# Five plain pairs instead of seven, one product packed into three PSUM banks, D folded into C and 7, and eight adds on GpSimd

## The chip, the cores and the metric

The kernel runs on one core of a Trainium2 chip. The metric is the time of one execution on the device in microseconds, lower is better. The span in a profile goes from the first to the last instruction of one profiled execution; the execution's own time is a little longer.

The engines are called as in the profile: PE (TensorE, matrix products, with PEld for its weight loads), DVE (VectorE), ACT (ScalarE), POOL (GpSimd) and SP (SyncE, which here only issues transfers). Every engine works through its own instructions in their order and waits on semaphores for the others.

## The reference

```python
def setup_inputs():
    batch, m, k, n = 16, 512, 1024, 768
    return {
        "input": np.random.randn(batch, m, k).astype(np.float32),
        "grad_output": np.random.randn(batch, m, n).astype(np.float32),
    }

def reference(input, grad_output):
    grad_weight = np.einsum('bmk,bmn->kn', input, grad_output)
    return grad_weight.astype(np.float32)
```

Both inputs are seen as matrices X of 8192 x 1024 and G of 8192 x 768, and the result is X transposed times G, 1024 x 768, in float32.

## The kernel before

**Tiles.** The 8192 rows are cut into 64 slabs of 128 rows, and two slabs make a pair, so there are 32 pairs (`u`, 0 to 31). The result is cut into four quadrants of 512 x 384: A (upper left), B (upper right), C (lower left), D (lower right). Each quadrant has four blocks of 128 x 384 (`q`, 0 to 3), so A2 is the third block of A. One product is a matmul of a 128x128 weight tile and a 128x384 moving tile in bf16, which adds into a PSUM bank.

**Two kinds of pairs** (`LOADS`, line 12). A plain pair `s` needs for each slab the four quadrants' four blocks, so 32 products in all. A pair `P` treats its two slabs and the two halves of X's and G's columns as 2 x 2 block matrices and multiplies them by Winograd's form of Strassen's scheme, with seven products instead of eight, so 28 products of the same size. These seven are named 1, 5, 6, 7, A, B and C; their results go to sums of their own (`macc` for 1, 5, 6, 7), and A, B and C share the sum with the plain pairs. D gets products from plain pairs alone. The scheme needs sums of operands: six DVE instructions a pair in bf16, three for X (`sum_x`, lines 183 to 187, tokens x0, x1, x2) and three for G (`sum_g`, lines 193 to 197, tokens g0, g1, g2). Before, pairs 0 to 5 and pair 31 are plain and 25 are `P`.

**Loads.** POOL issues nearly all loads before everything else, in the order of the pairs: G's tile (line 152), then X's (line 153), cast from float32 to bf16 on the way. Fourteen pairs fit at once. The first slabs come as float32 through SP and ACT and are rounded by DVE and ACT (line 201), so that PE can start early. Ahead of that a few warm-up matmuls (line 135) run on constants.

**Blocks and banks.** PSUM has eight banks, and a block in work holds one. There are 32 sums of 128 x 384, so blocks are carried in and out. `multiply` (line 277) runs some products of a block; `close` (line 297) takes a bank's sum to SBUF, by an ACT copy (token c, line 327), or by DVE (token v: a copy at line 329, or an add onto the sum so far at line 331); `fill` (line 265) has ACT copy a sum back into a bank (token f, line 274), after which products add onto it. The four blocks of A stay in banks 7, 4, 1 and 3 until near the end; the rest rotates over banks 0, 2, 5 and 6.

**The end.** The quadrants are put together from the products when a block is closed for the last time (lines 304 to 312): 6 takes 1, 7 takes 6, A takes 1, C takes 7; 5 is closed by two subtractions (lines 307 and 309), and B and D take what these leave. A finished quadrant block of 192 KB is stored by SP (line 320); the very last block, B3, lies in two banks, 256 and 128 columns, and its second part is stored through ACT's queue.

**What sets the order.** `PLAN` (line 17) is a list of tokens, computed ahead of time and written out. The loop at line 336 goes through it, and each engine gets its instructions in the order of the tokens. `C2@0.1` is one product of C2, opened in bank 0; `A1.3` three more of A1; `fC1@3` fills C1 into bank 3; `cB1` and `vB1` close B1; `x0.6` is the first X sum of pair 6; `r0` to `r4` are roundings. The token's place among the others is no clock: only the order on each engine and the semaphores count.

Of the kernel before, what the change touches and what calls it, by code (L numbers as in the profile page):

```python
# [11 lines left out]
LOADS = "ssssssPPPPPPPPPPPPPPPPPPPPPPPPPs"  # L12

PLAN = (
    "A0@7.1 A3@3.1 A1@4.1 C3@5.1 C2@0.1 C1@2.1 r0 cC3 C0@6.1 vC2 A2@1.1 cC1 D0@5.1 vC0 B0@0.1 cD0 D1@2.1 "
    "r1 r3 B3@6.1 r2 D3@5.2 vB0 r4 A1.1 A2.1 cD1 vB3 A3.1 B1@0.2 cD3 B2@2.2 vB1 D2@6.2 cB2 C0@5.1 C1@0.1 "
    "vD2 A0.1 fD0@2 A2.1 vC0 A3.1 fD1@6 A1.1 D0.2 vC1 C2@5.2 cD0 D1.2 vC2 C3@0.2 cD1 B0@2.2 vC3 B3@5.3 "
    "fB1@6 vB0 A0.2 fB2@0 vB3 B1.2 fC0@2 B2.2 cB1 C1@5.2 vB2 C0.2 fD2@6 A3.1 vC1 D3@0.2 cC0 D2.2 fC2@5 "
    "vD3 C3@2.1 A1.1 cD2 A2.1 vC3 C2.1 B0@0.1 D1@6.1 vC2 D0@2.1 vB0 fD2@5 A3.2 vD1 A1.2 fB0@0 D2.2 vD0 "
    "B1@6.2 cD2 B0.2 vB1 B2@2.2 cB0 B3@5.2 vB2 C0@6.2 fC1@0 A2.2 vB3 fC2@2 C1.2 vC0 C3@5.2 cC1 C2.2 vC3 "
    "fD0@6 A0.2 D1@0.4 vC2 D3@5.4 vD1 D0.4 vD3 C3@2.2 vD0 B3@5.2 C0@0.2 vC3 fC1@6 A3.2 vB3 fB2@2 A0.2 vC0 "
    "C1.2 fD2@5 B2.2 cC1 D2.2 vB2 C2@0.2 cD2 B0@6.2 vC2 fB1@2 A1.4 vB0 fC1@0 B1.4 C2@5.2 cB1 D2@6.2 vC2 "  # L30
    "C1.2 fD0@2 A2.4 vD2 fD3@5 vC1 fC3@6 D0.2 D3.2 vD0 C3.2 cD3 C0@0.2 vC3 B2@2.4 vC0 fB3@6 B0@5.4 vB2 "
    "fD1@0 B3.4 fC0@2 vB0 A3.1 g0.6 fB1@5 A3.3 vB3 A0.2 g1.6 A0.2 fC1@6 D1.1 g2.6 D1.3 A2.2 vD1 A1.3 x0.6 "
    "fC2@0 C0.3 C1.1 x1.6 C1.2 cC0 C2.1 x2.6 C2.2 cC1 C3@2.1 g0.7 C3.2 cC2 B1.3 fD0@6 vC3 D2@0.2 g1.7 cB1 "
    "D0.2 vD2 fD3@2 A2.1 A3.1 A0.1 g2.7 cD0 10@5.1 D3.2 c10 x0.7 11@0.2 cD3 12@6.2 v11 13@5.2 c12 50@2.1 "
    "x1.7 50.1 c13 51@0.2 x2.7 52@6.2 c50 g0.8 53@5.2 c51 70@2.2 v52 c53 A2.1 g1.8 A3.1 fB3@0 72@6.2 v70 "
    "73@5.2 c72 g2.8 B3.2 v73 63@2.2 cB3 B2@6.1 x0.8 B2.1 fC1@5 A1.2 v63 A0.2 71@0.1 x1.8 71.2 vB2 62@2.3 "
    "c71 x2.8 C1.2 c62 g0.9 60@6.3 cC1 61@2.1 g1.9 61.2 fB0@0 v60 10@5.2 c61 g2.9 B0.3 v10 fC3@6 C2@2.2 "
    "cB0 x0.9 C2.1 C3.3 fC0@5 vC2 A2.2 f52@0 C0.1 x1.9 cC3 C0.2 A3.1 x2.9 A3.1 cC0 12@2.1 g0.10 12.1 52.2 "
    "f63@5 v12 B1@6.3 c52 g1.10 63.2 f13@2 vB1 11@0.2 c63 A0.1 g2.10 13.2 v11 72@5.2 c13 x0.10 A1.2 f51@0 "
    "53@6.2 v72 A0.1 f70@2 A3.1 51.1 x1.10 f50@5 51.2 v53 70.3 c51 x2.10 50.2 f73@6 g0.11 50.1 B3@0.3 c70 "  # L40
    "v50 73.2 fB2@2 g1.11 73.1 vB3 A2.1 f10@5 B2.2 c73 g2.11 B2.1 10.1 x0.11 10.2 cB2 C1@0.3 c10 x1.11 "
    "62@6.2 f71@2 vC1 A3.1 A1.1 f61@5 A0.1 x2.11 71.2 f60@0 g0.12 71.1 61.3 v62 c71 60.1 g1.12 60.2 c61 "
    "B0@2.1 g2.12 fB1@6 B0.2 v60 11@5.2 vB0 B1.2 fC0@0 A2.1 x0.12 A2.1 cB1 A0.1 C0.3 fC2@2 v11 A3.1 fC3@6 "
    "A1.1 x1.12 C2.3 cC0 x2.12 13@5.2 f53@0 g0.13 13.1 C3.3 cC2 v13 53.2 f52@2 g1.13 53.1 vC3 12@5.3 c53 "
    "g2.13 52.3 f72@6 v12 63@0.2 x0.13 c52 63.1 72.3 f62@5 v63 A2.1 f51@2 A1.1 x1.13 62.2 c72 51.1 x2.13 "
    "51.2 f50@0 v62 73@6.3 c51 g0.14 50.3 f70@5 v73 A3.1 fB2@2 A0.1 70.1 g1.14 c50 70.2 g2.14 B3@6.3 c70 "
    "B2.1 x0.14 B2.2 10@5.3 vB3 cB2 C1@0.1 x1.14 C1.2 f60@6 v10 11@2.3 x2.14 60.2 f61@5 g0.15 60.1 A1.1 "
    "61.3 c60 vC1 A0.1 g1.15 71@6.3 c61 v11 B0@0.1 fB1@5 g2.15 B0.2 v71 A2.2 fC2@2 A3.1 x0.15 A3.1 f52@6 "
    "B1.3 vB0 C2.2 cB1 x1.15 C2.1 52.2 cC2 x2.15 52.1 C0@0.1 fC3@5 g0.16 C0.2 A1.1 c52 A0.1 vC0 C3.3 "
    "f12@2 g1.16 13@6.3 vC3 12.2 g2.16 f62@5 12.1 v13 53@0.3 c12 x0.16 62.3 f72@6 A1.1 v53 63@2.3 c62 "  # L50
    "x1.16 f50@0 72.4 v63 f51@5 50.1 g0.17 50.2 c72 70@2.1 x2.16 70.2 c50 g1.17 51.3 v70 73@6.2 g2.17 c51 "
    "73.1 B2@0.1 x0.17 fB3@2 B2.2 A2.2 fC1@5 v73 B3.3 x1.17 C1.3 vB2 cB3 10@6.2 x2.17 cC1 10.1 71@0.1 "
    "g0.18 f11@2 71.2 A3.2 v10 f60@5 11.1 g1.18 11.2 v71 60.3 c11 g2.18 61@6.3 c60 x0.18 A0.3 fC0@2 v61 "
    "B1@0.3 fB0@5 x1.18 C0.3 fC2@6 vB1 B0.2 cC0 x2.18 B0.1 C2.1 g0.19 f12@0 C2.2 C3@2.3 cB0 vC2 12.2 "
    "f62@5 g1.19 12.1 vC3 A1.2 c12 53@6.1 g2.19 53.2 f52@2 x0.19 13@0.4 v53 A3.2 52.1 x1.19 f72@6 52.3 "
    "v13 62.2 x2.19 c52 62.2 g0.20 73@0.3 c62 g1.20 63@2.4 f51@5 v73 72.1 g2.20 72.2 fC1@0 v63 51.3 c72 "
    "x0.20 A2.3 c51 70@2.1 x1.20 70.3 f71@5 x2.20 50@6.4 v70 C1.1 g0.21 C1.2 fB2@2 A0.2 v50 cC1 B2.2 "
    "g1.21 B2.2 fB3@6 g2.21 A1.2 cB2 B3.4 x0.21 71.3 cB3 B0@0.2 x1.21 c71 B0.1 10@6.2 x2.21 10.2 vB0 "
    "C2@2.2 g0.22 C2.1 f61@0 A3.2 vC2 11@5.3 g1.22 11.1 f60@2 61.4 v10 g2.22 60.4 v11 c61 x0.22 C0@6.4 "
    "f53@0 c60 12@5.1 x1.22 12.3 vC0 B1@2.2 x2.22 B1.2 g0.23 C3@6.4 v12 53.2 g1.23 53.2 vB1 A1.2 c53 vC3 "  # L60
    "52@5.3 f73@2 g2.23 13@0.2 x0.23 13.2 A2.3 v52 A0.1 x1.23 A0.2 f51@5 v13 A3.2 51.1 x2.23 51.2 g0.24 "
    "51.1 73.3 c51 g1.24 73.1 C1@6.1 g2.24 C1.2 c73 63@5.4 vC1 f72@2 70@0.1 x0.24 f71@6 70.2 72.5 v63 v70 "
    "f62@5 A1.2 x1.24 c72 71.2 g0.25 71.2 f50@0 62.1 x2.24 fB2@2 62.2 g1.25 62.2 c71 B2.1 g2.25 B2.3 c62 "
    "50.4 vB2 B0@6.1 x0.25 f10@2 B0.3 c50 C2@5.1 x1.25 C2.3 f11@0 vB0 10.2 x2.25 10.2 g0.26 11.4 c10 vC2 "
    "B3@6.2 f60@2 g1.26 B3.2 c11 g2.26 B3.1 60.4 vB3 fB1@0 61@5.2 fC0@6 x0.26 61.2 c60 B1.4 v61 12@2.1 "
    "x1.26 fC3@5 12.3 vB1 C0.2 g0.27 f53@0 C0.2 x2.26 C3.2 cC0 g1.27 C3.2 v12 53.3 cC3 g2.27 53.1 52@6.4 "
    "v53 A2.1 x0.27 f51@0 A2.3 v52 A3.3 x1.27 A3.1 f70@6 A0.2 x2.27 A0.2 g0.28 A1.3 13@2.1 g1.28 13.2 "
    "g2.28 13.1 C1@5.4 v13 51.4 f73@2 vC1 70.1 x0.28 f63@5 70.3 c51 73.1 x1.28 73.3 c70 x2.28 73.1 63.2 "
    "c73 g0.29 63.3 f72@2 50@0.1 g1.29 50.2 c63 g2.29 50.1 71@6.4 v50 f62@5 72.4 fB0@0 v71 62.1 x0.29 "
    "f11@6 62.3 c72 B0.1 x1.29 B0.3 c62 x2.29 11.4 fB2@2 vB0 fC2@5 B2.1 g0.30 B2.4 f10@0 v11 C2.4 vB2 "  # L70
    "f11@6 10.1 g1.30 f12@2 10.3 vC2 A2.1 g2.30 A2.2 c10 x0.30 12.4 f13@5 f10@0 x1.30 11.1 13.3 c12 v11 "
    "10.1 A3.1 f61@2 x2.30 A3.2 v13 f62@6 A1.3 v10 f63@5 61.5 f60@0 62.2 v61 60.5 v62 f71@2 A2.2 f72@6 "
    "v60 A3.2 A1.2 vA2 f70@0 A0.5 vA3 vA1 70.3 vA0 63.2 v70 f50@1 71.2 72.2 fC0@3 v63 50.2 f73@0 v71 C0.6 "
    "f51@4 v72 fC1@5 v50 51.3 f52@2 fC2@7 C1.5 vC0 fD0@6 v51 fB0@1 52.4 fD1@3 B0.4 vC1 fB1@4 C2.3 v52 "
    "fD2@5 B1.7 vB0 fB2@2 vC2 73.2 vB1 B2.3 v73 f53@1 D0.2 D1.2 fC3@4 vB2 53.4 vD0 C3.6 vD1 v53 fD3@0 "
    "fB3@2+7 D2.2 D3.2 vC3 B3.7 vD2 vD3 vB3 "
).split()


WARMUP = [("b", 512), ("f", 512), ("f", 512), ("b", 512)]  # L80
PAIRS_HELD = 14
SUMS_HELD = 10

MERGED = 2


@with_exitstack
def kernel(
# [6 lines left out]
    nc = tc.nc  # L95
# [155 lines left out]


    SHARED = {"A": "1", "B": "5", "C": "7", "D": "1", "6": "1", "7": "6"}

    done = {(p, q): 0 for p in streams for q in range(Q)}
    fresh = {(p, q): True for p in streams for q in range(Q)}
    closed = set()
    opened = {}
    used = {7}
    stores = [0]  # L260

    def bank(b):
        return psum.tile([P, 512], f32, name=f"bank{b}")

    def fill(p, q, b, b2):
        assert (p, q) not in opened and not fresh[p, q] and b in used
        src = sum_of(p, q)
        if b2 is None:
            parts = [(bank(b), 0, NH)]
        else:  # L270
            assert b2 in used
            parts = [(bank(b), 0, 256), (bank(b2), 256, NH)]
        for tile_, c0, c1 in parts:
            nc.scalar.copy(out=tile_[:, 0 : c1 - c0], in_=src[:, c0:c1])  # L274
        opened[p, q] = (parts, True)

    def multiply(p, q, b, n):
        first = (p, q) not in opened
        if first:
            opened[p, q] = ([(bank(b), 0, NH)], False)  # L280
            used.add(b)
        parts, carried = opened[p, q]
        for tile_, c0, c1 in parts:
            for j in range(n):
                at = done[p, q] + j
                stat, mov = operands(p, streams[p][at], q)
                nc.tensor.matmul(  # L287
                    tile_[:, 0 : c1 - c0],
                    stat,
# [7 lines left out]
    def close(engine, p, q):  # L297
# [34 lines left out]
        if final:  # L332
            closed.add((p, q))
# [51 lines left out]
```

## Time and profile before

| What | Value |
|---|---|
| Runs of the kernel | median 162.35 us, 162.21 to 162.44, three runs |
| The profiled execution's own time | 162.31 us |
| Its span | 160.5 us |
| Granted clock of PE | 1.00 throughout |
| Loads (HBM read 58.72 MB) | DMA engines full until about 141 us |
| POOL's load issues | 1.2 to 126.2 us, then nothing |
| ACT copies, fill and close | 0.48 us each from start to end |
| DVE add from a bank, 128x384 float32 | 0.55 us each |
| DVE sums of a `P` pair | 0.68, 0.42, 0.42 us (X) and 0.55, 0.35, 0.35 us (G) |
| Matmul of 384, 256, 128 columns | 0.326, 0.272, 0.219 us from start to end |
| Weight load | 0.098 us |
| Store of 192 KB by SP | 1.9 us from issue to landing |

Busy time counts an engine from an instruction's start to its end, with overlaps counted once. Instructions of one engine overlap: a matmul starts about half its own length after the one ahead of it. So what one more instruction costs is read from the distance between starts (or ends), not from the length of one. Where many instructions of one line follow each other, the timeline gives them as one row with a count.

### The profile page before, as it was taken

To read this page: it belongs to the slowest core of one execution; us is meant where nothing else is said; L and a number is where in the kernel's file an instruction comes from. 1 tells how busy PE (TensorE), PEld (TensorE's weight loads), DVE (VectorE), ACT (ScalarE), POOL (GpSimd) and SP (SyncE) were. 2 spreads that over 40 slices of the span, in tenths; PEclk is the share of its full clock that TensorE was granted. 3 is DMA by queue.
4 is the path that set the end of the run, shared out by engine and by line. 5 is a ranking of instruction groups with operands and counts; after the bars stand their busy time and mean duration, and the time that the engine had idled before them with its cause. 6 is when DMAs were issued, how large, how long until landed. Compare 5 with 4: busy or idle time off the path is not lost.

```text
span 160.5 us, 2776 instructions
## 1 busy us (share of the span) xinstructions
PE 155.3 (97%) x937; PEld 91.9 (57%) x937; DVE 142.7 (89%) x323; ACT 112.8 (70%) x253; POOL 34.8 (22%) x69
## 2 busy tenths in 40 slices
PE   8899999999999999999999999999999999999990
PEld 3355556556556656655655655665665665556560
DVE  0788986989999999999989998998899998989992
ACT  3779737749888999968777786534777368877730
POOL 7452222122221222222122222212222100000000
PEclk9999999999999999999999999999999999999999
DMA  5999999999999999999999999999999999924385
GB/s 176 295 213 213 210 216 213 213 213 212 213 212 212 213 213 214 210 214 213 215 214 213 213 212 212 213 212 214 213 210 213 215 212 214 212 43 157 137 294 196
DMA packets 12830, 33.40 MB, mean 208 GB/s; under 512 B 1424, under 2 KB 4624, under 8 KB 12816
## 3 DMA queue, kind: packets, MB, share of 16 engines
q0 software_dynamic: 9360, 28.64, 90.2%
q1 hardware_dynamic: 3024, 3.47, 6.3%
q10 hardware_dynamic: 432, 1.11, 1.8%
q8 instruction: 7, 0.11, 0.3%
q14 instruction: 7, 0.06, 0.1%
HBM read 58.72 MB, written 3.15 MB: 385 GB/s over the span
## 4 chain that ended last, share of the span: by engine, by line
DMA 48%; PE 44%; DVE 2%; issue 2%; POOL 1%; DVEq 0%; POOLq 0%
DMA xp<-in_input_dram 48%; PE bank L287 44%; POOL gp L157 1%; DVE acc L312 1%; DVE xe L183 0%; POOL xp L159 0%; DVE acc L331 0%; DVE macc L331 0%; DVEq L380 0%; DVE xe L185 0%; POOLq L153 0%; POOLq L369 0%; POOLq L152 0%
## 5 line engine op out<-in xcount | busy, mean ns | idle before, releaser
L287 PE MATMUL bank<-gp,xp 128*128 128x384 bf16 (+2 forms) x631 | 109.8, 324 | 0.6 <-DVE xp L201 0.6
L287 PEld LDWEIGHTS <-xp 128*128 128x128 bf16 x631 | 61.1, 98 | 42.5 <-DVE xp L201 1.3
L287 PE MATMUL bank<-ge,xe 128*128 128x384 bf16 x300 | 56.2, 326 | 0.1
L274 ACT COPY bank<-macc 128x384 f32<-128x384 f32 x71 | 33.6, 484 | 13.2 <-DVE macc L331 5.6
L287 PEld LDWEIGHTS <-xe 128*128 128x128 bf16 x300 | 29.3, 98 | 19.9 <-issue 0.6
L274 ACT COPY bank<-acc 128x384 f32<-128x384 f32 (+1 forms) x70 | 32.3, 479 | 9.1 <-DVE acc L329 5.5
L327 ACT COPY macc<-bank 128x384 f32<-128x384 f32 x61 | 28.6, 479 | 9.5 <-PE bank L287 8.1
L331 DVE TENSOR_TENSOR acc<-bank,acc 128x384 f32<-128x384 f32 x54 | 28.7, 552 | 2.8 <-PE bank L287 1.2
L153 POOL DMA_DIRECT2D xp<-in_input_dram x30 | 16.0, 532 | 53.3 <-DMA xp<-in_input_dram 28.0
L327 ACT COPY acc<-bank 128x384 f32<-128x384 f32 x45 | 21.4, 480 | 6.5 <-PE bank L287 6.0
L152 POOL DMA_DIRECT2D gp<-in_grad_output_dram x30 | 16.0, 533 | 37.1 <-DMA gp<-in_grad_output_dram 15.0
L331 DVE TENSOR_TENSOR macc<-bank,macc 128x384 f32<-128x384 f32 x41 | 22.5, 551 | 0.5 <-PE bank L287 0.2
L183 DVE TENSOR_TENSOR xe<-xp 128x1024 bf16<-128x1024 bf16 x25 | 17.1, 683 | 1.2 <-DMA xp<-in_input_dram 1.2
L329 DVE COPY acc<-bank 128x384 f32<-128x384 f32 x24 | 13.1, 553 | 3.0 <-PE bank L287 2.4
L193 DVE TENSOR_TENSOR ge<-gp 128x768 bf16<-128x768 bf16 x25 | 13.8, 550 | 0.0
L187 DVE TENSOR_TENSOR xp<-xp,xe 128x512 bf16<-128x512 bf16 x25 | 10.5, 419 | 0.4
L185 DVE TENSOR_TENSOR xe<-xe,xp 128x512 bf16<-128x512 bf16 x25 | 10.5, 418 | 0.3
L197 DVE TENSOR_TENSOR gp<-ge,gp 128x384 bf16<-128x384 bf16 x25 | 8.8, 352 | 0.3
L195 DVE TENSOR_TENSOR ge<-gp,ge 128x384 bf16<-128x384 bf16 x25 | 8.7, 350 | 0.2
L312 DVE TENSOR_TENSOR acc<-bank,macc 128x384 f32<-128x384 f32 (+2 forms) x17 | 8.0, 522 | 0.0
L329 DVE COPY macc<-bank 128x384 f32<-128x384 f32 x14 | 7.6, 552 | 0.4 <-PE bank L287 0.4
L201 DVE CAST gp<-gf 128x192 bf16<-128x192 f32 (+1 forms) x2 | 0.7, 360 | 4.9 <-DMA gf<-in_grad_output_dram 4.9
(17 smaller groups left out, 21.6 us busy)
## 6 DMA issues: line engine op xcount, KB each, us to landing
xp<-in_input_dram POOLq DMA_DIRECT2D x30, 512.0 KB, 16.9
gp<-in_grad_output_dram POOLq DMA_DIRECT2D x30, 384.0 KB, 16.7
out_dram<-acc SPq DMA_DIRECT2D x12, 192.0 KB, 1.9
xf<-in_input_dram ACTq DMA_DIRECT2D x2, 512.0 KB, 5.0
gp<-in_grad_output_dram POOLq DMA_DIRECT2D x3, 192.0 KB, 6.6
out_dram<-acc SPq DMA_DIRECT2D x6, 96.0 KB, 1.7
xp<-in_input_dram POOLq DMA_DIRECT2D x2, 256.0 KB, 8.0
gf<-in_grad_output_dram SPq DMA_DIRECT2D x2, 192.0 KB, 4.2
```

Of the source, the lines that this page charges most:

```text
L152: nc.gpsimd.dma_start(out=gp, in_=G[rows, :].rearrange("(p m) n -> p m n", m=2))
L153: nc.gpsimd.dma_start(out=xp, in_=X[rows, :].rearrange("(p m) k -> p m k", m=2))
L183: nc.vector.tensor_sub(out=xe[:, 0:2, :], in0=x[:, 1::-1, :], in1=x[:, 3::-2, :])
L185: nc.vector.tensor_sub(out=xe[:, 2, :], in0=xe[:, 0, :], in1=x[:, 0, :])
L187: nc.vector.tensor_add(out=x[:, 1, :], in0=x[:, 2, :], in1=xe[:, 2, :])
L193: nc.vector.tensor_add(out=ge[:, 0:2, :], in0=g[:, 0:2, :], in1=g[:, 1::2, :])
L274: nc.scalar.copy(out=tile_[:, 0 : c1 - c0], in_=src[:, c0:c1])
L287: nc.tensor.matmul(tile_[:, 0 : c1 - c0], stat, mov[:, c0:c1], start=first and j == 0, stop=True, skip_group_check=True,)
L312: nc.vector.tensor_add(out=dst[:, c0:c1], in0=b, in1=sum_of(SHARED[p], q)[:, c0:c1])
L327: nc.scalar.copy(out=dst, in_=b)
L329: nc.vector.tensor_copy(out=dst, in_=b)
L331: nc.vector.tensor_add(out=dst, in0=b, in1=dst)
```

## The change

- `LOADS`: pairs 0 to 4 are plain, 5 to 31 are `P`. There is no plain pair at the end.
- A's four blocks lie side by side in banks 5, 6 and 7 (`R`): A0 in bank 5, A1 in the last 128 columns of bank 5 and 256 of bank 6, A2 in 256 of bank 6 and 128 of bank 7, A3 in bank 7. A product of A1 or A2 is now two matmuls. The rest rotates over banks 0 to 4 until A is closed, and after that over more.
- D is finished after the five plain pairs. At one of the closes of each block of C and 7 (token k) DVE adds D to C or subtracts it in 7, in place of a copy. The second subtraction of a 5 block then gives D's result, which is stored at once.
- A block may be opened anew in an empty bank though its sum is in SBUF, also while its former bank is not yet closed; the close then adds onto the sum.
- POOL adds eight shared sums with `tensor_add` in SBUF: tokens p (62, 60, C2: the shared sum goes in ahead of the last close) and q (A1, A0, C1, A3, B2: after an ACT copy out of the bank, and the store follows). They stand behind all loads in POOL's order. The built program has an instruction that loads POOL's code ahead of the first of them.
- The warm-up is 33 bf16 matmuls, one of 512 columns and 32 of 128, in place of two bf16 and two float32 ones of 512.
- The first four stores, not three, are cut in two; the last block B3 lies in one bank and is stored as a whole by SP.
- The whole `PLAN` is new.

```diff
-LOADS = "ssssssPPPPPPPPPPPPPPPPPPPPPPPPPs"
+LOADS = "sssssPPPPPPPPPPPPPPPPPPPPPPPPPPP"
...
 PLAN = (
-    "A0@7.1 A3@3.1 A1@4.1 C3@5.1 C2@0.1 C1@2.1 r0 cC3 C0@6.1 vC2 A2@1.1 cC1 D0@5.1 vC0 B0@0.1 cD0 D1@2.1 "
...
-    "fB3@2+7 D2.2 D3.2 vC3 B3.7 vD2 vD3 vB3 "
+    "A0@R.1 A3@R.1 C1@0.1 C2@1.1 C0@2.1 cC1 C3@3.1 r0 A1@R.1 cC2 vC0 A2@R.1 D2@4.1 cC3 B0@0.1 B1@1.1 vD2 "
...
+    "g1.31 A2.3 g2.31 12.2 x0.31 12.2 A1.1 A3.1 c12 A2.1 x1.31 11.1 cA1 A0.1 vA2 p62 10@4.1 cA3 72.2 v10 61.1 "
+    "c11 62@6.2 f71@7 62.1 v61 qA1 62.2 cA0 71.1 x2.31 71.1 f52@4 60@1.1 v62 60.1 p60 f13@5 60.2 v71 60.1 "
+    "fC1@6 52.2 v72 f73@3 13.1 qA0 13.1 v60 C1.1 f63@2 C1.1 70.1 v52 70.1 c13 C2@7.2 pC2 fC0@1 C2.1 63.2 f50@5 "
+    "v70 C0.2 cC1 C0.1 vC2 50.1 fB2@4 50.1 qC1 50.1 v63 50.1 fC3@7 73.2 vC0 B2.1 f51@2 B2.2 qA3 v73 fB1@6 B2.1 "
+    "C3.2 v50 cB2 C3.1 51.1 fB0@0 51.1 qB2 51.2 fB3@3 vC3 51.1 B0.1 f53@1 B0.1 v51 B0.3 53.3 vB0 53.1 B1.2 v53 "
+    "B1.3 B3.3 vB1 B3.2 vB3 "
 ).split()
...
-WARMUP = [("b", 512), ("f", 512), ("f", 512), ("b", 512)]
+WARMUP = [("b", 512)] + 32 * [("b", 128)]
...
+HALVED = 4
...
-    SHARED = {"A": "1", "B": "5", "C": "7", "D": "1", "6": "1", "7": "6"}
+    SHARED = {"A": "1", "B": "5", "C": "7", "6": "1", "7": "6"}
...
+    def resident_parts(q):
+        if not resident:
+            resident.update({b: bank(b) for b in (5, 6, 7)})
+        a, b, c = (resident[i] for i in (5, 6, 7))
+        return [
+            [(a, 0, 0, NH)],
+            [(a, NH, 0, 128), (b, 0, 128, NH)],
+            [(b, 256, 0, 256), (c, 0, 256, NH)],
+            [(c, 128, 0, NH)],
+        ][q]
...
+    def close(engine, p, q, queue):
+        parts, carried = opened[p, q].pop(0)
+        final = last(p, q) and not opened[p, q] and p not in "1D"
...
+            if engine == "c":
...
+                nc.scalar.copy(out=to, in_=b)
+            elif engine == "k":
...
+                d = sum_of("D", q)[:, c0:c1]
+                (nc.vector.tensor_add if p == "C" else nc.vector.tensor_sub)(out=to, in0=b, in1=d)
...
+            elif final and p == "5":
...
+                nc.vector.tensor_sub(out=to, in0=b, in1=sum_of("6", q)[:, c0:c1])
+                d = sum_of("D", q)[:, c0:c1]
+                nc.vector.tensor_sub(out=d, in0=b, in1=sum_of("7", q)[:, c0:c1])
+                store("D", q, c0, c1, queue)
...
+            elif carried:
+                nc.vector.tensor_copy(out=to, in_=b)
+            else:
+                nc.vector.tensor_add(out=to, in0=b, in1=to)
...
+    def add_shared(p, q, prepare, queue):
...
+        dst = sum_of(p, q)
+        nc.gpsimd.tensor_add(out=dst, in0=dst, in1=sum_of(SHARED[p], q))
...
+            store(p, q, 0, NH, queue)
```

## The prediction

> **What bounds the kernel now.** I read the page first, then the busy time by stretch, then the ends of single matmuls, then the chain of waits.
>
> ```profile
> PE 155.3 (97%) x937; PEld 91.9 (57%) x937; DVE 142.7 (89%) x323; ACT 112.8 (70%) x253; POOL 34.8 (22%) x69
> DMA  5999999999999999999999999999999999924385
> ```
>
> TensorE (PE) is busy 97% of the span; of its 937 matmuls 6 are warm-up, and 931 are the 924 products, of which seven are cut in two. The DMA engines are full for 34 of 40 slices, until about 141 us. Busy is not yet bound, so the stretches:
>
> ```profile
> core 0: us, PE busy (x) PEld busy (x) DVE busy (x) ACT busy (x) POOL busy (x), PEclk, DMA share, GB/s
> 50.00:60.00 10.00, 10.00 (x63) 6.00 (x62) 9.92 (x25) 9.25 (x22) 2.12 (x4) 1.00 1.07 212
> ...
> 100.00:110.00 10.00, 10.00 (x64) 6.05 (x62) 9.88 (x24) 4.37 (x10) 2.38 (x5) 1.00 1.07 213
> ```
>
> VectorE (DVE) is at 99% in both, ScalarE (ACT) at 92% and at 44%, and PE runs at the same rate. So PE itself sets the pace. Its pace in the timeline of PE alone:
>
> ```profile
> 91.88 3.58 PE L287 MATMUL bank<-ge,xe 128*128 128x384 bf16 x21
> ```
>
> One matmul takes 0.326 us from start to end (page), so 20 steps take 3.58 - 0.326, or 0.1627 us each; I use 0.1625, which also fits longer rows. Then the stretches from four moments to the end; the number behind x is how many matmuls still end after that moment:
>
> ```profile
> 5.54:165.00 159.46, 151.12 (x930) 0.99 0.97 201
> 155.72:165.00 9.28, 1.14 (x14) 0.91 0.29 100
> 156.48:165.00 8.52, 0.38 (x7) 0.91 0.27 92
> 156.87:165.00 8.13, 0.00 (x0) 0.90 0.27 94
> ```
>
> By moving the left end in steps of 0.01 us: the first product ends at 5.53, the last whole one at 155.71, seven of 256 columns at 156.47, seven of 128 at 156.86. So 151.33 us pass after the first, and 923 x 0.1625 is 149.99: **all stalls of PE together are 1.33 us** (0.5 before 8.2 us, 0.3 around 15 to 17, 0.31 at 84.7, 0.13 at 142.5, crumbs elsewhere).
>
> ```profile
> 64.61 17.76 DMA xp<-in_input_dram
> 82.37 0.02 issue
> 82.40 0.69 DVE xe L183
> ...
> 84.41 70.98 PE bank L287 x435
> 155.39 0.36 DVE acc L312
> ```
>
> The chain shows the second limit: at 82.40 DVE's first sum of a pair waited for that pair's load, and PE stalled behind it at 84.7. From there PE holds the chain, and the last adds and stores end it. After the last matmul (156.86) come 3.64 us of tail.
>
> **The change, part by part.**
>
> *Products.* Seven plain pairs become five: 7 x 32 + 25 x 28 = 924 products become 5 x 32 + 27 x 28 = 916. Eight fewer at 0.1625 us: **-1.30 us**, straight on PE's path.
>
> *A in three banks.* A1 and A2 lie across two banks, so each of their 74 products becomes a 128-column and a 256-column matmul. The tail of before has just these forms: seven of 256 take (156.47 - 155.71)/7 = 0.1086 us each, seven of 128 take 0.39/7 = 0.0557, each with its own weight load; together 0.1643, or 0.0018 more than a whole product. 74 - 7 more of them: **+0.12 us**. A rule speaks against that: the Trainium skill, "TensorE: Matmul & The Clock Gate", section "Back-to-back issue gap", gives about 81 ns for each 128-column matmul in a real stream of weight loads and matmuls. The seven rows here, such a stream, say 56 ns; by that page the sum would be 74 x 0.025 = 1.9 us worse; I go by the rows.
>
> *Other banks.* The blocks that are carried in and out now rotate over five banks, not four. Counted in the order of PE's products, from the last product of a bank's visit to the first product after its next fill: in the middle of the kernel (50 to 96 us) the median is 12 products (1.95 us) before and 16 (2.60 us) after, the least of the whole order 7 and 9 (1.14 and 1.46 us). A close and a fill need about 1.2 us (0.48 each, 0.18 of matmul latency, waits). So each visit has more room. Worth 0 to -0.5 us (the stalls of the start, where banks are turned fastest); I take 0.
>
> *Closes and fills.* Copies by ACT: closes go from 106 to 130, fills from 141 to 177; bank operations of DVE (v, k, second subtractions) from 166 to 148, sums from 150 to 162. D costs nothing at its end: its four closing adds go, because C and 7 take it in when they are closed anyway (k). For ACT I use steps between starts in its timeline:
>
> ```profile
> 53.60 0.48 ACT L327 COPY macc<-bank 128x384 f32<-128x384 f32 x1
> 53.98 0.49 ACT L274 COPY bank<-macc 128x384 f32<-128x384 f32 x1
> ...
> 57.07 1.31 ACT L274 COPY bank<-macc 128x384 f32<-128x384 f32 x3
> ```
>
> After a close the next copy starts 0.375 us later, after a fill (1.31 - 0.48)/2 = 0.415. ACT's work rises from 106 x 0.375 + 141 x 0.415 = 98 to 122 us. It lies beside PE, but not evenly: while PE goes from 25.3 to 86.0 us the new order has 70 closes and 79 fills, 59.0 us in 60.7, **97%** (the old order 75% there). DVE at 0.47 a bank operation and 2.3 a pair of sums is at 90% there (92% before). What hides ACT is the room above. Without an idle moment it fits, and DVE at 99% held PE up nowhere in 50 to 60 us, so I take 0; the other end is rival 1.
>
> *Loads.* Their order and size stay, so their landings do: each issue on POOL waits for the transfer eight before it, and so the xp issue at 95.42 us marks the xp of pair 20. Its first sum stands after 546 products in the new order, 93.9 us without a stall, so 1.4 us of stalls (or of waiting on DVE) belong there by then; in the old order 94.1 and 1.3. So the loads hold both orders to nearly the same place, and I keep the 1.33 us of stalls, which I do not expect to shrink. Behind pair 24 the new order is slack against them.
>
> *Start.* 33 short matmuls in place of two bf16 and two fp32 ones. The first bf16 one of before took 0.59 us; 32 at 0.056 end near 3.2 us, at twice that near 4.9, both before the first operand's rounding frees PE at 5.19. 0 either way, unless PE then starts slow: up to 16 first products at double time, +2.6 us as the outer end; nearest are the first products of before, at full pace, so 0.
>
> *GpSimd.* Eight adds of 128x384 from p62 (11.2 us before PE's end) to qB2 (3.6 us before it), behind the last load issue on POOL. In the trace POOL is idle from 126 us on, which covers a code reload that the built order has before the first add (no row shows its length; the cover is 17 us, to p62, and beyond it every microsecond delays the adds). An add has no row: DVE does it in 0.545 us (lower end); twice that plus POOL's 0.53 for a DMA issue is 1.6 (upper end). I take 1.0, nearest to DVE's row. v60, in DVE's strict order, needs p60, which stands behind qA1: two adds in 2.1 us, so up to 1.05 each cost nothing. Behind a late v60 stand v52, vC2 and all later closes; on SP, whose stores go in order, all stores behind that of a late q. The Trainium skill, "GPSIMD Engine Reference", section "Elementwise — side-by-side cycle accounting", has such an add 1.96 times slower than on DVE; by that estimate it is 1.07 us and the cost 0 to 0.1; no run here shows it.
>
> *Tail.* DVE has 12.6 us of work from x0.31, which stands 12.35 us before PE's end, and may end 0.7 after it: just enough, as in before, whose last seven DVE operations ran without a gap. The last add is 0.545 us on 384 columns instead of two parts, ending about 0.75 us after PE instead of 0.54, and stores 192 KB (1.9 us to landing) where 64 KB (2.1) went: between 0 and +0.3, **+0.15 us**.
>
> *Sum.* -1.30 + 0.12 + 0.15 = -1.03. The profiled execution took 162.31 us (span 160.5), the median of the runs is 162.35: **161.3 us**.
>
> **Rivals.** (1) *ACT becomes the bound* (slower). Place: 25 to 96 us. Nothing in before shows ACT above 92.5% busy. If it cannot pass 93%, 59.0 us need 63.4, 2.7 more than PE; 0.5 of the stalls run alongside, so +2.2: **163.5**. It decides from 95% downwards, 59.0/(60.7 + 0.5 + 1.0). For it: ACT waits in order for closes by PE; against it: the longer turns, and fewer fills that follow their own close (8, 22 before). (2) *GpSimd's adds are slow.* At 1.4 us each v60 waits 0.7 us, and vC2, four adds behind qA1's start, 1.5; DVE has 0.5 to spare: +1.0, **162.3**. (3) *128-column matmuls are held up by their weight loads*, 98 ns each in the profile, where loads do not overlap in a mixed stream: 74 x (0.098 - 0.056) = +3.1, **164.4**; the seven rows speak against it. (By the Trainium skill's 81 ns, in "TensorE: Matmul & The Clock Gate", it would be 163.2.) (4) *Fewer stalls*: five banks remove the 0.5 us of the start and DVE takes up late loads in its slack, **160.7**.
>
> **How the numbers follow.** Chances: forecast 0.54 (161.0 to 161.8), ACT 0.18, GpSimd 0.13, 128-column 0.04, fewer stalls 0.11. The range takes in the last and most of ACT's: 160.6 to 163.5. A measurement here tells 0.2% (0.32 us) from no change. Faster: forecast, fewer stalls and a few mild GpSimd cases, 0.68; same: most of GpSimd's, 0.10; slower: 0.22.
>
> **What would show it.** PE's products at 0.1625 us with stalls of about 1.3 us in all, last matmul near 155.7; splits at 0.164 a pair; ACT over 95% busy from 25 to 90 us without a gap in PE; POOL adds near 1 us, the first well after its reload; tail near 3.8 us. PE waiting for ACT's fills in 25 to 96 us, DVE waiting for POOL behind 145, or a first stretch at half pace would make it wrong.

## The result, and the profile after

The changed kernel takes 162.9 us (median of 5 runs, 162.64 to 163.12), the kernel before 162.27 on the same chip (5 runs, 162.18 to 162.44). The ratio is 1.0034, with a 95% interval of 1.0022 to 1.0046: **0.55 us slower**, where 1.0 us less was forecast. The time lies inside the stated range of 160.6 to 163.5, but that is luck: no rival of the prediction named what made it. The profiled execution took 162.90 us, its span 161.1 (before: 162.31 and 160.5).

Page of the changed kernel, engines and the DMA row in 40 slices:

```profile
PE 154.7 (96%) x1023; PEld 96.7 (60%) x1023; DVE 141.3 (88%) x317; ACT 129.6 (80%) x313; POOL 42.8 (27%) x77
DMA  5999999999999999999999999999999999912396
```

PE is 0.6 us less busy in a span that is 0.6 us longer. The last four digits of the DMA row, the stores, are 2, 3, 9 and 6 where they were 4, 3, 8 and 5: the stores come later and closer together. The two stretches of before, and the one in which ACT was to be nearly full:

```profile
50.00:60.00 10.00, 10.00 (x69) 6.29 (x67) 9.64 (x24) 9.95 (x26) 2.25 (x5) 1.00 1.07 212
100.00:110.00 10.00, 10.00 (x70) 6.33 (x68) 9.12 (x22) 6.80 (x18) 2.59 (x5) 1.00 1.07 213
25.00:86.00 61.00, 61.00 (x406) 38.26 (x405) 57.63 (x132) 60.45 (x151) 14.84 (x28) 1.00 1.07 213
```

ACT (the fourth pair of columns) is at 9.95 of 10.00 and at 60.45 of 61.00, and PE (the first) has no gap. Then PE alone, from three moments to the end:

```profile
5.64:165.00 159.36, 150.57 (x990) 0.99 0.97 201
157.22:165.00 7.78, 0.01 (x1) 0.87 0.33 119
157.23:165.00 7.77, 0.00 (x0) 0.87 0.33 119
```

The first product ends at 5.65, the last matmul at 157.24 (with the modelled ends, to 0.02 us). That gives the ledger of the two spans. Its first two rows are counted at the prediction's steps per product, and the stalls of PE are what is left:

| Term, us | Forecast | Measured |
|---|---|---|
| Eight products fewer | -1.30 | -1.30 |
| A1 and A2 in two parts | +0.12 | +0.12 |
| End of the first product (5.53, now 5.65) | 0 | +0.12 |
| All stalls of PE (1.33, now 2.77) | 0 | +1.44 |
| From the last matmul to the end (3.64, now 3.86) | +0.15 | +0.22 |
| Sum | -1.03 | +0.60 |

From 20 to 90 us the changed kernel does 430 products in 70 us, 0.1628 us each, parts and all, so the steps hold. One row is far off. Its stalls, by steps of the left end: 0.30, 0.59, 0.17 and 0.26 us at 145.0, 147.2, 149.2 and 150.9, together 1.32, where the kernel before had no gap behind 142.5; 0.53 at 95.8, where before had 0.31 at 84.7; the rest at the start. So of the 1.44 us more, 1.2 lie behind 142 us and 0.2 at the one wait for a load. The first product's 0.12 is within what executions differ by: in other profiles with the new warm-up it ends anywhere from 5.55 to 5.79, and once at 6.25. The chain of waits of the changed kernel, near its end (start, length, what):

```profile
139.98 3.98 PE bank L320 x30
...
143.98 0.48 ACT macc L339
144.46 0.45 ACT acc L339 x2
...
144.94 0.63 DVE acc L353 x2
...
145.59 0.48 ACT acc L339
146.07 0.38 ACT macc L339
146.46 0.40 ACT bank L301
...
146.89 1.95 PE bank L320 x11
```

For three microseconds the chain leaves PE. ACT copies A1 out in its two parts (144.46), DVE then adds A2's two parts (144.94), ACT then copies A3 (145.59), then comes what stands behind that in ACT's order, the close c11 and the fill f71@7, and only then PE goes on with 71 in bank 7 (146.89). ACT had waited 1.46 us before 143.98, so it had time, but earlier.

**Theory 1.** A's blocks share banks: A1's part and A0 in 5, parts of A1 and A2 in 6, A2's part and A3 in 7. The program lets one engine at a time use a bank, whatever the columns, so PE's last product of A0, ACT's cA1, DVE's vA2 and ACT's cA3 form a line, and the fill that PE needs stands behind it. The Trainium skill, "PSUM — Partial Sum Buffer", section "PSUM bank collisions raise a hardware error", says that any two engines on one bank (in the same 32 partitions) must be kept apart by semaphores, at different addresses too; the waits here agree (DVE waited 0.61 us for ACT's part in bank 6, ACT 0.69 for DVE's in bank 7).

**Theory 2.** GpSimd's adds hold up DVE. DVE and POOL of the changed kernel in the same moments (start, length):

```profile
146.96 0.85 DVE L190 TENSOR_TENSOR xp<-xp,xe 128x512 bf16<-128x512 bf16 x1
```

```profile
146.53 1.00 POOL L369 TENSOR_TENSOR acc<-acc,macc 128x384 f32<-128x384 f32 x1 [0.99 <-ACT macc L339]
147.49 1.18 POOL L369 TENSOR_TENSOR macc<-macc 128x384 f32<-128x384 f32 x1
```

x2.31, a sum of two operands in SBUF, takes 0.85 us instead of 0.42, and the POOL add that starts within it 1.18 instead of 1.00. DVE's adds out of a bank beside the same POOL adds keep their 0.55. The Trainium skill, "SBUF — State Buffer", section "Who interferes with whom", says that a DVE operation with two SBUF inputs shares a read port with GpSimd's reads and that one blocks the other; these rows agree. The stalls at 149.2 and 150.9 follow behind it.

### The profile page after: what moved, and what is told of

Same layout as the page of the kernel before. It is cut to its first block, busy times and chain, and to the rows that moved or that the text cites. A ratio compares the mean times of both kernels' runs of the same rounds, so it can differ in the third digit from the quotient of the medians.

```text
span 161.1 us, 3022 instructions
## 1 busy us (share of the span) xinstructions
PE 154.7 (96%) x1023; PEld 96.7 (60%) x1023; DVE 141.3 (88%) x317; ACT 129.6 (80%) x313; POOL 42.8 (27%) x77
## 4 chain that ended last, share of the span: by engine, by line
PE 72%; DMA 13%; ACT 10%; DVE 1%; issue 1%; ACTq 0%
PE bank L320 72%; DMA xp<-in_input_dram 11%; ACT bank L301 5%; DMA xf<-in_input_dram 3%; ACT macc L339 3%; ACT acc L339 2%; DVE acc L353 1%; DVE macc L357 0%; DVE gp L200 0%; DVE xp L204 0%; ACTq L339 0%
## 5 line engine op out<-in xcount | busy, mean ns | idle before, releaser
L320 PE MATMUL bank<-gp,xp 128*128 128x384 bf16 (+2 forms) x666 | 107.3, 308 | 1.3 <-DVE xp L204 0.8
L320 PE MATMUL bank<-ge,xe 128*128 128x384 bf16 x324 | 62.4, 326 | 0.4 <-ACT bank L301 0.4
L301 ACT COPY bank<-macc 128x384 f32<-128x384 f32 x91 | 42.9, 494 | 10.3 <-DVE macc L359 3.6
L301 ACT COPY bank<-acc 128x384 f32<-128x384 f32 x86 | 41.0, 500 | 2.4 <-DVE macc L359 1.0
L339 ACT COPY acc<-bank 128x384 f32<-128x384 f32 (+1 forms) x65 | 30.1, 484 | 3.6 <-PE bank L320 2.4
L359 DVE TENSOR_TENSOR acc<-bank,acc 128x384 f32<-128x384 f32 x33 | 17.5, 553 | 2.0 <-PE bank L320 1.6
L357 DVE COPY macc<-bank 128x384 f32<-128x384 f32 x28 | 15.5, 554 | 1.8 <-PE bank L320 1.0
L359 DVE TENSOR_TENSOR macc<-bank,macc 128x384 f32<-128x384 f32 x30 | 16.5, 550 | 0.4 <-PE bank L320 0.2
L369 POOL TENSOR_TENSOR macc<-macc 128x384 f32<-128x384 f32 x2 | 2.2, 1088 | 18.2 <-ACT macc L339 18.2
L369 POOL TENSOR_TENSOR acc<-acc,macc 128x384 f32<-128x384 f32 x6 | 5.9, 1001 | 1.9 <-ACT macc L339 1.0
```

Of the source, the lines that this page charges most:

```text
L301: nc.scalar.copy(out=tile_[:, at : at + c1 - c0], in_=src[:, c0:c1])
L320: nc.tensor.matmul(tile_[:, at : at + c1 - c0], stat, mov[:, c0:c1], start=fresh, stop=True, skip_group_check=True,)
L339: nc.scalar.copy(out=to, in_=b)
L357: nc.vector.tensor_copy(out=to, in_=b)
L359: nc.vector.tensor_add(out=to, in0=b, in1=to)
```

## The experiments

Ratios are to the kernel before, run on the same chip beside them; its median there was 162.41 (first four), 162.36 (next four), 162.44 (next four) and 162.28 (last four).

### One wait at a time

`e1_a0_first`, A0's product ahead of A1's close:

```diff
-cA1 A0.1 vA2 p62
+A0.1 cA1 vA2 p62
```

> One token moved: A0's last product stands ahead of the ACT copy of A1, so PE no longer waits at 144.7 us for that copy to leave bank 5, which A0 and A1 share. Theory 1 (the four blocks of A lie in three banks, a bank is left to one engine at a time, and so the closes of A run one after the other across PE, ACT and DVE): the 0.30 us stall of PE at 144.7 goes, but the fill of 71 into bank 7 still comes at 146.8, so most of it moves there; 162.6 to 162.9, against 162.9 for the changed kernel. Rival A (the stall of A0 is a loss by itself, in series with the others): 162.6. Rival B (ACT and DVE simply have too much work at the end): 162.9.

163.38 us, ratio 1.0058 [1.0039, 1.0076]: 0.4 us worse than the change itself. None of the three expectations has that. A0's 0.30 us goes, but PE stalls 0.60 and 0.67 at 145.9 and 147.3, the first of them for vA2's part in bank 6: 1.27 together, where the change has 0.89. The line from cA1 to the end of f71 is as long as before (2.48 us), but cA1 now waits for A0's product too and starts 0.76 us behind c12's start, not 0.38. So the whole line comes 0.4 us later, which is what the run lost.

`e2_x2_early`, the second sum of pair 31 ahead of the GpSimd adds:

```diff
-A2.1 x1.31 11.1 ... 71.1 x2.31 71.1 f52@4
+A2.1 x1.31 x2.31 11.1 ... 71.1 71.1 f52@4
```

> One token moved: the last X sum of pair 31 (x2.31) stands directly behind x1.31, where DVE was idle for 0.6 us, and no longer beside GpSimd's second add. Theory 2 (an add on GpSimd and a DVE sum with two operands in SBUF hold each other up: this sum took 0.85 us there and 0.42 elsewhere): its length falls to 0.42, the later closes 62 and 60 and the fills behind them come 0.4 us earlier, the stalls of 0.17 and 0.26 us at 149 and 150.7 shrink; 162.5 to 162.7. If the sum's length does not matter: 162.9.

162.86 us, 1.0027 [1.0017, 1.0037]. DVE of this version:

```profile
144.13 0.42 DVE L190 TENSOR_TENSOR xp<-xp,xe 128x512 bf16<-128x512 bf16 x1
```

The sum takes 0.42 us, and the stalls at 149 and 151 are gone: theory 2 is right on what made them. PE ends 0.66 us earlier (156.57); 0.43 of that are the two stalls, and 0.23 this execution had gained before 144.8 us already, at the start and the loads. Yet the median fell by 0.1 us at most. That stayed open until the last runs.

`e3_a2_reversed`: A2's two parts are closed in the other order, bank 7 first, and f71@7 stands directly behind cA3.

```diff
-for tile_, at, c0, c1 in parts:
+for tile_, at, c0, c1 in parts[::-1] if (p, q) == ("A", 2) else parts:
...
-cA3 72.2 v10 61.1 c11 62@6.2 f71@7 62.1
+cA3 f71@7 72.2 v10 61.1 c11 62@6.2 62.1
```

> A2's two parts are closed in the other order, bank 7 first, and the fill of 71 into bank 7 stands directly behind the close of A3, ahead of c11. Then A3's copy no longer waits for A2's part in bank 6, which waits for A1's copy. Theory 1: ACT's wait of 0.69 us ahead of cA3 goes, the fill of 71 is there about 0.8 us earlier, and the stall of 0.59 us at 146.9 falls below 0.2; 162.3 to 162.5. Rival B (too much work on ACT and DVE at the end, whatever the order): the stall turns up at the next fills; 162.8 or more.

162.71 us, 1.0018 [1.0006, 1.003], 0.25 us better than the change, between what theory 1 and rival B had. No trace of it can be set beside the others, so which stalls went is not shown.

`e4_all_three`, the three together:

> All three moves together, no work added or left out. Theory 1 with theory 2: the stalls of PE between 144 and 151 us, 1.3 in the changed kernel, fall below 0.5; 161.9 to 162.1, which is 0.2 to 0.4 below the kernel before. Rival B: 162.5 or more.

162.68 us, 1.0016 [1.0004, 1.0029], in rival B's range by its number. PE stalls 0.60 at 146.3 for A2's part in bank 6 and 0.30 at 147.8. Three repairs of single links are worth 0.3 us: with one link eased, the next one in line holds PE. Rival B (too much work at the end, whatever the order) stands until the next run.

### The whole line earlier

`e5_a_early`: A0, A1 and A3 get their last products first, cA1 and cA3 use the time in which ACT was idle, A2 comes last, x2.31 is early.

```diff
-g1.31 A2.3 g2.31 12.2 x0.31 12.2 A1.1 A3.1 c12 A2.1 x1.31 11.1 cA1 A0.1 vA2 p62 10@4.1 cA3 72.2 v10 61.1 c11 62@6.2
+g1.31 A0.1 A1.1 A3.1 g2.31 cA1 12.2 x0.31 12.2 cA3 11.1 A2.4 c12 x1.31 x2.31 p62 c11 vA2 10@4.1 72.2 v10 61.1 62@6.2
...
-71.1 x2.31 71.1 f52@4
+71.1 71.1 f52@4
```

> The end of A in another order, no work added or left out: A0, A1 and A3 get their last products first, ACT copies A1 and then A3 out while PE works on 12 and 11, and only then come A2's last four products, its close by DVE, and 10; x2.31 stands behind x1.31. In this order no product and no copy finds a shared bank in use by another engine, and ACT uses the 1.5 us for which it waited ahead of c12. Theory 1 (shared banks at the end of A, and only they, cost the stalls of 1.3 us between 144 and 151 us) with theory 2 (0.4 us of the last X sum): these stalls fall below 0.4 us, 161.8 to 162.1 against 162.9 for the changed kernel and 162.3 to 162.4 for the one before. Rival B (too much work on ACT and DVE at the end): 162.5 or more, with the stalls at later fills.

**161.91 us**, 0.9967 [0.9956, 0.9979]: 1.1 us below the change and 0.5 below the kernel before. Stretches of the changed kernel and then of this one:

```profile
144.00:146.00 2.00, 1.87 (x14) 1.05 (x12) 1.39 (x4) 1.31 (x5) 1.00 (x1) 1.00 0.00 0
146.00:148.00 2.00, 1.57 (x10) 0.85 (x9) 1.54 (x4) 2.00 (x6) 1.47 (x2) 1.00 0.31 98
```

```profile
144.00:146.00 2.00, 2.00 (x19) 1.43 (x17) 1.97 (x6) 1.48 (x5) 1.34 (x2) 1.00 0.00 0
146.00:148.00 2.00, 2.00 (x14) 1.22 (x13) 1.87 (x5) 2.00 (x6) 2.00 (x3) 1.00 0.47 151
```

PE (first pair of columns) goes from 1.87 and 1.57 to 2.00 and 2.00, DVE (third) from 1.39 and 1.54 to 1.97 and 1.87. PE's last matmul ends at 156.04, 1.2 us earlier, and the tail is 3.86 us as in the change. So the waits at 144 to 151 us, both theories together, cost the change 1.1 us, and an order of the same tokens avoids them. With no work taken away, rival B falls. How much of it each theory has in this order was not run apart.

`e6_a_early_b3`: the same, with B3 in two banks as in the kernel before (`fB3@3+4`, `B1.3 vB1 B3.5 vB3`).

> The same, and the last block B3 is filled into two banks, 256 and 128 columns, closed in two parts and stored through two queues, as the kernel before has it. If the longer tail (3.86 us after the last matmul against 3.64) comes from the last add on 384 columns and its 192 KB store: 0.2 us below the run without it. If the tail is set by the stores ahead of it: no difference.

162.31 us, 1.0005 [0.9989, 1.002]: 0.4 worse than without, against every expectation. Its one profile is of an execution of 163.75 us that had lost 1.3 us against `e5_a_early` by 139 us already: its first products came 0.32 us apart until 9.8 us, twice the usual step. So it doesn't show the 0.4, and the cause was left to the last runs.

### GpSimd's adds, and the warm-up

`e7_adds_dve`, the eight adds on DVE:

```diff
-nc.gpsimd.tensor_add(out=dst, in0=dst, ...
+nc.vector.tensor_add(out=dst, in0=dst, ...
```

> One part of the change undone: the eight shared sums are added by DVE in the same places, GpSimd adds nothing. Theory 2 alone would have it gain 0.4 us at the last X sum. But DVE has 97% of its time taken in the last 13 us, and gets eight times 0.46 to 0.55 us more: 3.7 to 4.4 us, of which it can take in 0.5; 165.5 to 166.5 if DVE then sets the end. If the adds on GpSimd bring nothing that DVE could not do beside its other work: 162.9 or less.

164.95 us, 1.0165 [1.015, 1.018]: 2.05 us worse than the change, less than the 165.5 expected. Eight adds at 0.465 us are 3.7 us of DVE's time; its last add ends 2.4 us later (160.24), as it had 1.1 us of idle time between 142 and 148 to fill, and x2.31, with no add on GpSimd, takes 0.42 us again. Giving the adds to GpSimd is worth 2 us in this order.

`e8_old_warmup`, the changed kernel with the warm-up of before:

```diff
-WARMUP = [("b", 512)] + 32 * [("b", 128)]
+WARMUP = [("b", 512), ("f", 512), ("f", 512), ("b", 512)]
```

> One part of the change undone: the warm-up is the old one, two bf16 and two float32 matmuls. In the profiles the first product ends at 5.65 us after and 5.53 before, and the stalls below 10 us are about the same. If the warm-up has no part in it (operands came later by chance): 162.9, as the changed kernel. If the short matmuls delay or slow the first products: 162.6 to 162.8.

164.12 us, 1.0108 [1.0094, 1.0121], 1.2 us worse than the change, against both expectations, though PE and DVE end 0.3 us earlier (156.95 and 157.55). All of it is behind them: the tail is 5.55 us. Stretches of this version (last two columns: DMA share, GB/s):

```profile
155.00:156.00 1.00, 1.00 (x8) 0.61 (x7) 1.00 (x3) 0.00 (x0) 0.00 (x0) 1.00 0.97 349
156.00:157.00 1.00, 0.94 (x6) 0.36 (x4) 0.93 (x3) 0.00 (x0) 0.00 (x0) 1.00 0.24 78
157.00:158.00 1.00, 0.00 (x0) 0.00 (x0) 0.54 (x1) 0.00 (x0) 0.00 (x0) 1.00 0.70 252
```

In the midst of the last stores the DMA engines stand almost still for a microsecond: SP's fifth last store leaves at 156.92, at 155.95 in the changed kernel, because SP needs 1.68 us for the issue ahead of it, where 0.4 is usual. What else used the DMA engines, by queue, from 154.7 to 155.0 us:

```profile
q1 hardware_dynamic: 71, 0.10, 98.1%
q8 instruction: 1, 0.02, 33.6%
```

and in the changed kernel, from 149.6 to 149.9, the only packet there:

```profile
q8 instruction: 1, 0.02, 24.3%
```

The instruction queue moved eight packets of 16 KB in the changed kernel's execution, one per 17 to 20 us. PE runs 1023 matmuls and 1023 weight loads; 8 x 16,384 bytes over 2046 is 64 bytes each, so a packet is 256 PE instructions, if all of it is PE's. The old warm-up has 27 matmuls and 27 weight loads fewer by the two pages (996 of each), and the last packet comes 5.0 us later, into the dense stores; 54 instructions of 256 make some 4 us of that; an expectation below counts 61, which no page shows. The packet takes 1.6 us there (33.6% of sixteen engines' 0.3 us) on one DMA engine, and 0.9 to 1.2 elsewhere (24.3% is 1.17). A store is spread over all sixteen, and four stores then took 4.0 to 4.2 us to land, where 2.2 is usual. In the changed kernel too the packet meets stores, the first ones: SP's issue at 150.03 takes 1.32 us. But there it has caught up by 154.3, where SP waits for the next sum again. **Theory C**: this packet's place makes the 1.2 us. Two runs on it:

`e11_nine_wide`, the changed kernel with `WARMUP = 9 * [("b", 512)]`, 48 PE instructions fewer and no float32:

> The changed kernel with nine products of 512 columns as PE's warm-up (no fp32 ones, and 48 PE instructions fewer than with one of 512 and 32 of 128). In the trace the instruction queue loads one packet of 16 KB per some 20 us of PE's work, 1.6 us long among the stores and 0.9 to 1.2 us elsewhere; the last came 10.05 us ahead of the last store's end in the changed kernel, where few stores were under way, and 6.4 us ahead in the run with the old warm-up, in the midst of the final stores, where SP's next store then came 1.3 us late. Theory C (that packet's place makes the 1.2 us of the old warm-up): 48 instructions of the 256 that a packet would hold at 64 bytes move it by 48/256 of 20 us, 3.8 us, to about 153.6 us, behind the first of the dense stores at 152.9: 163.6 to 164.2. Rival (the fp32 products of the old warm-up cost it, by the clock or otherwise): 162.8 to 163.0.

163.99 us, 1.0099 [1.0086, 1.0112]; the packet came at 153.7, as worked out, and the DMA share in the stretch from 155 to 156 us was 0.08.

`e12_early_old_warmup`, `e5_a_early` with the old warm-up:

> The version that beat both (A's closes early, second sum of the last pair early; 161.9) with the old warm-up, 61 PE instructions fewer. Theory C: the last packet of code moves from 148.4 to about 153.4 us, where this kernel's stores are dense from 152 us on, and the gain of some 1.0 to 1.3 us is lost: 162.8 to 163.3. Rival (the old warm-up's loss belongs to the changed kernel's late tail alone): 161.8 to 162.0, since the first product comes 0.1 us earlier.

163.38 us, 1.0053 [1.0039, 1.0067]: 1.4 us more than `e5_a_early` by the ratios. The packet came at 153.9, 5.4 us later; a stretch of this version:

```profile
155.00:156.00 1.00, 1.00 (x7) 0.43 (x5) 1.00 (x3) 0.00 (x0) 0.00 (x0) 1.00 0.04 6
```

A share of 0.04 is less than one engine of sixteen. PE and DVE end as in `e5_a_early` (156.1 and 156.7). Theory C holds: in all three versions PE and DVE end at most 0.05 us later than with the new warm-up, the packet comes 4 to 5 us later, and the time is lost behind them. The float32 matmuls are not needed for it, as `e11_nine_wide` has none.

### The loads

`e9_two_loads_out` and `e10_before_loads_out`, the changed kernel and the kernel before without the loads of pairs 10 and 11:

```diff
+if u in (10, 11):
+    nc.gpsimd.memset(gp, 1.0)
+    nc.gpsimd.memset(xp, 1.0)
+else:
     nc.gpsimd.dma_start(out=gp, ...
     nc.gpsimd.dma_start(out=xp, ...
```

> The changed kernel with the four loads of pairs 10 and 11 left out: GpSimd fills their tiles with ones instead, so the output is not the reference's; 2 of 30 pair loads, about 3 us of the DMA engines' time, go. Every profile of this kernel's family shows one wait of PE for a load, of 0.5 to 0.7 us, at a place that moves (95.8 us in the changed kernel's profile, 57.2, 39.3 and 7.4 us in others). Theory 1 (the loads pace the order once, before and after the change alike, and the change's loss is at 144 to 151 us): that wait goes, 0.3 to 0.6 us, so 162.3 to 162.6, and the tail's waits stay. Rival (the new order runs nearer to the loads than the old one, and that is the change's loss): 0.8 us or more, 162.1 or below, while the same edit in the kernel before gives nothing.

> The kernel before with the same four loads left out (ones instead, so the output is not the reference's). Theory 1: as much as in the changed kernel, 0.3 to 0.6 us, 161.8 to 162.1. Rival (only the new order runs near the loads): nothing, 162.3 to 162.4.

162.79 us (1.0031 [1.0019, 1.0043]) and 162.48 (1.0003 [0.9993, 1.0014]): nothing in either, where theory 1 had 0.3 to 0.6 us in both and the rival 0.8 in the first. The wait for a load at 95.8 us is gone from the first one's profile, but the start there is 0.3 us slower. So the medians don't show that the change added a cost of waiting for loads, nor the 0.5 us that such a wait takes in single profiles.

### The last stores

Open was why `e2_x2_early` gained almost nothing and `e6_a_early_b3` lost. Kernel before, then `e2_x2_early` (DMA share and GB/s last):

```profile
154.00:155.00 1.00, 1.00 (x8) 0.60 (x7) 1.00 (x4) 0.22 (x2) 0.00 (x0) 1.00 0.77 277
156.00:157.00 1.00, 0.86 (x12) 0.65 (x9) 1.00 (x3) 0.00 (x0) 0.00 (x0) 1.00 0.29 105
```

```profile
154.00:155.00 1.00, 1.00 (x8) 0.61 (x7) 1.00 (x3) 0.00 (x0) 0.00 (x0) 1.00 1.03 367
156.00:157.00 1.00, 0.57 (x4) 0.12 (x2) 0.93 (x3) 0.00 (x0) 0.00 (x0) 1.00 1.02 366
```

The stores of before have gaps; those of `e2_x2_early` run from 153 us without one. SP issues them 0.49 us apart, and they land 0.53 apart, so each takes a little longer to land than the one ahead: 1.9 us at 152.0, 2.4 at the last. Four versions with two of them left out, D0's and D2's (that part of the output isn't written; all is computed):

```diff
 def store(p, q, c0, c1, engine):
+    if p == "D" and q in (0, 2):
+        return
```

> The version with the last pair's second sum early, and two of its late stores left out (blocks D0 and D2, 192 KB each, so that part of the output is not written; everything is computed). From 153 us on its DMA engines ran without a gap at some 366 GB/s, and its span ended 3.6 us behind DVE's last addition, against 3.1 in the kernel before, whose late stores left gaps. Theory S (the dense stores set this version's end, which is why 0.66 us less on PE and DVE was worth 0.1): the end comes down to DVE's end and some 3.1 us, 0.4 to 0.5 us: 162.3 to 162.5. Rival (the end is that of PE and DVE, and its profile was of a good execution): 162.8 to 162.9.

> The version with A's closes early and B3 in two banks, and the same two stores left out. Its one profile, of its slowest execution, showed a span that ended 4.2 us behind DVE's last addition. Theory S: the dense stores took B3's gain and the 0.4 us that it lost against the version without; without two of them 161.6 to 161.9. Rival (B3's two banks cost PE or DVE 0.4 us, by its smaller products): 162.2 to 162.3.

> The version with A's closes early (161.9), and the same two stores left out. Its span ended 3.26 us behind DVE's last addition. Theory S: its stores began 1 us earlier and hold its end by 0.1 to 0.2 us at most: 161.7 to 161.9. Rival (the stores hold the end of all of this family, one 192 KB store for one, 0.5 us): 160.9 to 161.4.

> The changed kernel with the same two stores left out. Its span ended 3.28 us behind DVE's last addition. Theory S: the change's loss is PE's and DVE's waits at 144 to 148 us, and the stores hold its end by 0.1 to 0.2 us: 162.7 to 162.9. Rival (the denser stores are the change's loss): 161.9 to 162.4.

| Version | With all stores | Two left out | Change of the ratio |
|---|---|---|---|
| `e2_x2_early` | 162.86, 1.0027 | 162.03, 0.9985 [0.9975, 0.9995] | -0.0042 (0.7 us) |
| `e6_a_early_b3` | 162.31, 1.0005 | 161.75, 0.9968 [0.9955, 0.9981] | -0.0037 (0.6 us, 0.5 by the medians) |
| `e5_a_early` | 161.91, 0.9967 | 161.67, 0.9963 [0.995, 0.9976] | -0.0004 |
| changed kernel | 162.9, 1.0034 | 162.94, 1.0042 [1.0029, 1.0055] | +0.0008 |

Theory S holds for the first two, though `e2_x2_early` came 0.3 us lower than expected. In its profile with all stores, the span is 0.37 us shorter than the changed kernel's, 0.23 of which it had before 144.8 us: of the 0.43 us that PE and DVE gained, 0.3 are lost in a longer tail. With one store more at the end (`e6_a_early_b3`) the stores set the end too. In `e5_a_early` the dense stores begin a microsecond sooner (at 152), and it keeps its gain; without the two stores it gains 0.1 us more at most.

For the changed kernel itself the run is weak. One stretch of `e2_x2_early` and one of the changed kernel, both without the two stores:

```profile
155.00:156.00 1.00, 1.00 (x8) 0.61 (x7) 1.00 (x3) 0.00 (x0) 0.00 (x0) 1.00 0.63 227
155.00:156.00 1.00, 1.00 (x8) 0.59 (x6) 1.00 (x4) 0.00 (x0) 0.00 (x0) 1.00 1.01 363
```

The first has a gap (DMA share 0.63), the second none (1.01): there SP waited until 152.69 for a sum and then issued almost without a pause, so its last stores stayed as dense as with all of them. That the time didn't fall therefore doesn't show that the stores cost the changed kernel nothing. They can cost it 0.5 us at most: its last store leaves 0.1 us behind DVE's last add and lands 2.3 us later, where 1.9 is usual without a queue. That the waits of PE and DVE cost 1.1 us is shown by `e5_a_early`, whose tail is as long. SP's order is not written in `PLAN`, and with two stores less it differs a little, so the sizes are rough to some tenths.

## Why the prediction was wrong, point by point

- **Products, splits**: right, -1.30 and +0.12. The 128-column matmuls kept their 0.056 us among the others, the 256-column ones took 0.109, and rival 3 falls. The 81 ns of the Trainium skill ("TensorE: Matmul & The Clock Gate", section "Back-to-back issue gap") do not show.
- **ACT**: right. It is at 99% from 25 to 86 us, and PE has no gap; rival 1 falls. The room for a close and a fill that was counted was enough. Only the chain of this one execution runs over ACT from 63.5 to 77.0 us, to the load that PE waits for at 95.8; whether ACT set that load's place is not shown.
- **Other banks: the step that failed.** It counted the room between one visit of a bank and the next, for the five banks that rotate, and took the stalls of PE as unchanged at 1.33 us. It did not look at the place where the resident banks 5, 6 and 7 are handed over to 62, 71 and 13. There the blocks share banks, so closes that before lay side by side in four banks of their own stand in one line: 0.30 + 0.59 us. The line could have been read in the order on record: cA1, vA2, cA3, and f71@7 behind them.
- **GpSimd**: the add was taken at 1.0 us and measured 1.00 (the estimate by the Trainium skill, "GPSIMD Engine Reference", section "Elementwise — side-by-side cycle accounting", was 1.07); the code reload was covered, since POOL waited 18.2 us for its first operand; v60 was not late. Rival 2 falls by length. What was missed is that an add also slows what runs beside it: 0.43 us on x2.31, and 0.17 + 0.26 of stalls behind it.
- **Loads**: no cost of the change, as forecast. The stall expected near 95 us came at 95.8, in part by luck: in other profiles of the new order a wait of that size stands at 39 or 57 us.
- **Start**: 0 forecast, +0.12 at the first product, within what executions differ by. The short matmuls took 0.107 us until 4.1 us and 0.057 behind, and in the profile of `e6_a_early_b3` the first products ran at half pace until 9.8 us: the half pace that the prediction had as its outer end occurs, in single executions, and took some 1.3 us there. What no step saw: the many short warm-up matmuls also moved a code packet from the midst of the stores to their beginning, worth 1.2 us. With the warm-up left as it was, the change would have been 1.8 us slower than before (1.0108).
- **Tail**: +0.15 forecast, +0.22 measured, of which 0.06 lie ahead of the end of DVE's last add and the rest in the last store. That the stores would run without a gap and could hold back work saved on PE was not in the prediction.

The forecast of 161.3 was for an order without the new waits. Such an order exists and takes 161.91. Its profiled execution (161.67) is 0.4 us above the forecast: 0.18 at the first product, 0.18 in stalls (1.51, not 1.33) and 0.07 in the tail. The median's other 0.2 was not taken apart.

## What to carry to other kernels

When blocks are packed across banks, list for each shared bank the engines in the order in which they use it; that line, not the room in the rotation, is what the hand-over cost here, and it belongs where the closing engines are idle. Repairing single links of the line gained little; moving the whole of it gained 1.1 us. Where the last stores run without a gap, work taken off PE at the end is worth only as much as the stores begin earlier, and a change in the number of PE's instructions, even in a warm-up, moves code loads that can hit those stores.

## What was not expected of the hardware

- Code comes in packets of 16 KB on a DMA queue of its own, here every 17 to 20 us, one per 256 PE instructions by the count above, each on one DMA engine for 0.9 to 1.2 us. Among dense stores it took 1.5 to 1.6 us, and the time grew by 1.1 to 1.4 us (three kernels).
- A DVE sum with both operands in SBUF took 0.85 us instead of 0.42 beside GpSimd's adds, one of which took 1.18 instead of 1.00.
- Stores of 192 KB with nothing else to move were issued by SP 0.49 us apart and landed 0.53 to 0.54 apart, some 366 GB/s, so the time to land grew from 1.9 to 2.4 us.
